# Gate and up by seven Strassen products for each pair of blocks, with half of the conditioning on TensorE, in a two-layer fp32 encoder

## The chip, the cores and the metric

The kernel runs on one core of a Trainium2 chip, once for each launch. The metric is the device time of that launch in microseconds; less is better. Five engines work beside each other, each through its own queue in order: TensorE (PE in the profile; the loads of its stationary operand are PEld), VectorE (DVE), ScalarE (ACT), GpSimd (POOL) and SyncE (SP), which here issues the DMA transfers. They meet only at semaphores.

## The reference, cut to what matters

Two layers over 1024 tokens of width 1024. Each has attention (layer 0, called A, windowed; layer 1, called B, dilated), then a SwiGLU feed-forward part (FFN) with 2816 hidden columns. The conditioning gives each layer six vectors of 1024 numbers (shift, scale and gate for each of the two parts).

```
cond = jax.nn.silu(c)
for i in range(DEPTH):
    mod = (cond @ ada_w[i] + ada_b[i])[:, None, :]
    sh1, sc1, g1, sh2, sc2, g2 = jnp.split(mod, 6, axis=-1)
    h = rmsnorm(x, norm_mix[i]) * (1 + sc1) + sh1
    y = windowed_gqa(...) if i % 2 == 0 else dilated_attention(...)
    x = x + g1 * y
    h = rmsnorm(x, norm_ffn[i]) * (1 + sc2) + sh2
    gate, up = jnp.split(h @ ffn_w_in[i], 2, axis=-1)
    x = x + g2 * ((jax.nn.silu(gate) * up) @ ffn_w_out[i])
return rmsnorm(x, final_norm)
```

## The kernel before

**Numbers.** Every matrix product has fp32 operands, and each is split into two fp32r parts, a high part (a rounding copy) and a low part (what the copy left). A product of a 128x128 block of weights with a 128x512 block of activations is then three matmuls into one PSUM bank (`acc3`, L284 high by high, L285 high by low, L286 low by high). `split_w` splits weights: ACT writes the high half (L180), POOL subtracts it for the low half (L181). Activations are split by ACT and DVE.

**Tiles.** x and h lie transposed, features on partitions, as 8 tiles of 128 features by 512 tokens for each half t of the tokens. The hidden columns are 22 blocks f of 128. For one f and one half, gate and up are 24 matmuls each (`up`, L421). Each f of `down` gives 24 matmuls to each half, in 8 tiles d; blocks of two f (one and three at the ends) share a PSUM bank, and DVE adds the tile to x (`residual`, L354). Down and attention use "d" banks of PSUM, FFN has six of its own beside two.

**Stages.** A start (norm of x, conditioning chunks 0 and 1 of layer 0); a stretch called PRE here (82 to 165 us), in which TensorE makes the last queries, keys and values while DVE forms chunks 2, 3 and 4 (`ada_steps`, L153: one 128x1024 multiply-add for each k; L167 sums over the partitions); attention A (165 to 430), 32 units, each with scores (L490, L491), softmax on DVE and ACT, transposes of the probabilities by TensorE (L532) and the product with the values (L526), into which a hand-written rate (`weave`, `tick`) puts fill work: the queries of half 1, the out-projection, norm and first gate and up of half 0. Then a transition (430 to 625): out-projection of half 1, its norm, gate and up of blocks 1 and 2 for half 0 as cover (`EARLY_A` 3), chunk 5; then FFN A to 1220, in which the 48 accumulations of layer 1's conditioning run on DVE in the background (`step`, one for each tile of gate or up). Attention B, its transition (`EARLY_B` 4) and FFN B repeat this. In `down` of the last block DVE squares the tiles as they come and the next norm starts half by half.

**Norm.** `rms` sums the squares over partitions with four one-column fp32 matmuls (L226), takes a Newton root, and spreads it with four 128-column matmuls (L244). `modulate` then makes each h tile: DVE scales (L256), ACT shifts and rounds (L257), DVE or POOL makes the low part (L262, L260).

**Weights.** `plan` lists the weight tiles in order of use; `weight` fetches ahead as far as there are slots ("w" tiles, two in `main`, a third in FFN). The order on each engine is set when the program is built, by a scheduler that simulates the program and may put instructions of independent pieces in another order than written; pools with few buffers set what can run ahead.

## Time and profile before

| | us |
|---|---|
| median of 3 runs | 2411.71 |
| lowest and highest run | 2411.21, 2413.84 |
| the profiled execution | 2411.33 |
| its span in the trace | 2409.5 |

So 1.8 us of the profiled execution lie outside the span. Below, "busy" is the time in which an engine's datapath worked, "idle before" the gap ahead of an instruction on its engine, and the engine behind an arrow is the one whose semaphore ended that gap. TensorE's matmuls are pipelined, so a matmul's own duration (about 0.39 us for 512 columns) is longer than the distance from one to the next; where matmuls are counted, the distance is what counts. PEclk is the granted clock of TensorE as a share of 2.4 GHz.

### The profile page before, as it was taken

To read this page: it belongs to the slowest core of one execution; us is meant where nothing else is said; L and a number is where in the kernel's file an instruction comes from. 1 tells how busy PE (TensorE), PEld (TensorE's weight loads), DVE (VectorE), ACT (ScalarE), POOL (GpSimd) and SP (SyncE) were. 2 spreads that over 40 slices of the span, in tenths; PEclk is the share of its full clock that TensorE was granted. 3 is DMA by queue.
4 is the path that set the end of the run, shared out by engine and by line. 5 is a ranking of instruction groups with operands and counts; after the bars stand their busy time and mean duration, and the time that the engine had idled before them with its cause. 6 is when DMAs were issued, how large, how long until landed. Compare 5 with 4: busy or idle time off the path is not lost.

```text
span 2409.5 us, 28051 instructions
## 1 busy us (share of the span) xinstructions
PE 2256.8 (94%) x10484; PEld 1863.5 (77%) x10484; DVE 1282.8 (53%) x2265; ACT 881.3 (37%) x1749; POOL 751.4 (31%) x483
## 2 busy tenths in 40 slices
PE   6799898988999999999989999797999999999997
PEld 5687676767788888888879878576788888888886
DVE  8869999578533333333362577786633332222325
ACT  4549887332111111111242788673411111111111
POOL 4525453453122122222233344344431212222210
PEclk9899998999999999999999999898999999999998
DMA  7441123666411111111234765736321111111101
GB/s 281 150 144 36 40 84 132 214 205 219 158 60 39 50 44 53 44 53 44 79 121 155 197 189 179 212 89 202 96 70 53 51 46 53 53 53 44 53 18 70
DMA packets 131224, 248.83 MB, mean 103 GB/s; under 512 B 39312, under 2 KB 66576, under 8 KB 130064
## 3 DMA queue, kind: packets, MB, share of 16 engines
q1 hardware_dynamic: 131088, 247.05, 32.1%
q8 instruction: 82, 1.34, 0.2%
q14 instruction: 54, 0.44, 0.1%
HBM read 214.20 MB, written 30.70 MB: 102 GB/s over the span
## 4 chain that ended last, share of the span: by engine, by line
PE 71%; DVE 16%; DMA 6%; issue 3%; ACT 3%; POOL 1%; SPq 1%; DVEq 0%; ACTq 0%; POOLq 0%
PE ps_d L284 22%; PE ps_d L285 22%; PE ps_d L286 22%; DMA ada_w<-in_ada_w 3%; DVE ada_acc L153 3%; DVE p L493 2%; DVE pp L535 2%; PE ps_o L526 1%; PE ps_t L532 1%; DVE ht L256 1%; DVE p L510 1%; DVE h L262 1%; DMA ml_all<-sd 1%; PE ps_s L491 1%; PE ps_s L490 1%
## 5 line engine op out<-in xcount | busy, mean ns | idle before, releaser
L284 PE MATMUL ps_d<-h,w 128*128 128x512 f32 x1968 | 780.8, 399 | 22.4 <-ACT w L180 11.1
L285 PE MATMUL ps_d<-h,w 128*128 128x512 f32 x1968 | 779.2, 396 | 11.4 <-DVE h L262 9.9
L286 PE MATMUL ps_d<-h,w 128*128 128x512 f32 x1968 | 775.9, 395 | 3.8 <-POOL w L181 3.8
L181 POOL TENSOR_TENSOR w<-raw,w 128x1024 fp32r<-128x1024 f32 (+1 forms) x178 | 431.2, 2424 | 758.7 <-ACT w L180 745.9
L284 PEld LDWEIGHTS ps_d<-h,w 128*128 128x128 f32 x1968 | 374.8, 191 | 96.3 <-ACT w L180 13.7
L285 PEld LDWEIGHTS ps_d<-h,w 128*128 128x128 f32 x1968 | 376.6, 191 | 84.3 <-DVE h L262 12.8
L286 PEld LDWEIGHTS ps_d<-h,w 128*128 128x128 f32 x1968 | 375.3, 191 | 84.7 <-POOL w L181 5.8
L401 DVE TENSOR_TENSOR u<-silu,ps_d 128x512 f32<-128x512 f32 x88 | 60.4, 686 | 607.6 <-PE ps_d L286 591.1
L354 DVE SCALAR_TENSOR_TENSOR x<-ps_d,mod,x 128x512 f32<-128x512 f32 x368 | 270.3, 747 | 149.2 <-PE ps_d L286 149.2
L180 ACT ACTIVATE w<-raw 128x1024 fp32r<-128x1024 f32 (+1 forms) x178 | 185.6, 1046 | 361.2 <-PE ps_d L286 295.3
L284 PE MATMUL ps_d<-act,wo 128*128 128x512 f32 x704 | 275.4, 391 | 8.9 <-DVE x L354 4.8
L286 PE MATMUL ps_d<-act,wo 128*128 128x512 f32 x704 | 274.3, 390 | 0.0
L285 PE MATMUL ps_d<-act,wo 128*128 128x512 f32 x704 | 274.2, 390 | 0.0
L181 POOL TENSOR_TENSOR wo<-raw,wo 128x1024 fp32r<-128x1024 f32 x44 | 105.6, 2399 | 432.7 <-ACT wo L180 425.3
L180 ACT ACTIVATE wo<-raw 128x1024 fp32r<-128x1024 f32 x44 | 46.7, 1060 | 382.8 <-PE ps_d L286 340.2
L284 PEld LDWEIGHTS ps_d<-act,wo 128*128 128x128 f32 x704 | 132.2, 188 | 39.0 <-DVE x L354 6.6
L286 PEld LDWEIGHTS ps_d<-act,wo 128*128 128x128 f32 x704 | 132.2, 188 | 27.5
L285 PEld LDWEIGHTS ps_d<-act,wo 128*128 128x128 f32 x704 | 132.3, 188 | 26.9
L403 DVE TENSOR_TENSOR act<-u,act 128x512 fp32r<-128x512 f32 x88 | 124.8, 1418 | 47.3 <-ACT act L402 47.1
L153 DVE SCALAR_TENSOR_TENSOR ada_acc<-ada_w,cond,ada_acc 128x1024 f32<-128x1024 f32 x70 | 117.2, 1674 | 49.0 <-DMA ada_w<-in_ada_w 48.3
L402 ACT ACTIVATE act<-u 128x512 fp32r<-128x512 f32 x88 | 55.0, 625 | 218.2 <-DVE u L401 218.1
L490 PE MATMUL ps_s<-kh,q 128*128 128x384 f32 (+3 forms) x320 | 104.0, 329 | 21.5 <-DVE stat L493 11.6
(168 smaller groups left out, 2656.3 us busy)
## 6 DMA issues: line engine op xcount, KB each, us to landing
raw<-in_ffn_w_in SPq DMA_DIRECT2D x102, 512.0 KB
ada_w<-in_ada_w SPq DMA_DIRECT2D x80, 512.0 KB
raw<-in_ffn_w_out SPq DMA_DIRECT2D x44, 512.0 KB
raw<-in_b_w_q SPq DMA_DIRECT2D x24, 512.0 KB
qd<-qo SPq DMA_DIRECT2D x48, 256.0 KB
h<-in_ada_w SPq DMA_DIRECT2D x8, 1024.0 KB
raw<-in_a_w_out SPq DMA_DIRECT2D x16, 512.0 KB
q<-qd SPq DMA_DIRECT2D x16, 512.0 KB
```

Source lines behind the costliest of these rows:

```text
L153: nc.vector.scalar_tensor_tensor(acc, w, s, acc, op0=ALU.mult, op1=ALU.add)
L180: self.nc.scalar.activation(w[:, 0], raw, AF.Copy)
L181: self.nc.gpsimd.tensor_tensor(w[:, 1], raw, f32(w[:, 0]), op=ALU.subtract)
L284: mm(ps, lhsT=w[0], rhs=x[0], start=first, stop=False)
L285: mm(ps, lhsT=w[0], rhs=x[1], start=False, stop=False)
L286: mm(ps, lhsT=w[1], rhs=x[0], start=False, stop=last)
L354: self.nc.vector.scalar_tensor_tensor(x, ps, self.mod[:, layer, c * 8 + d:c * 8 + d + 1], x, op0=ALU.mult, op1=ALU.add)
L401: nc.vector.tensor_tensor(u, s, up, op=ALU.mult)
L402: nc.scalar.activation(act[:, 0, halves(t)], u, AF.Copy)
L403: nc.vector.tensor_tensor(act[:, 1, halves(t)], u, f32(act[:, 0, halves(t)]), op=ALU.subtract)
L490: nc.tensor.matmul(ps[:, lo:hi], lhsT=qs[g], rhs=kh, start=True, stop=False)
L493: nc.vector.tensor_tensor_reduce(pt[g][:, lo:hi], ps[:, lo:hi], bias[g][:, lo:hi], -1.0, -NEG if sink is None else sink[1][:, g:g + 1], op ...
```

## The change

**Seven products.** From block 2 on, two blocks f and f+1 are taken together. For gate (and again for up) the result is a 2 by 2 matrix: block f or f+1 by token half 0 or 1; the contraction over 1024 features is cut into two halves of four tiles. That is a 2 by 2 matrix product, which was 8 products of 12 matmuls and becomes 7 (`seven`). The sums of weights that it needs (L502 to L505) are made by DVE in place in the raw tiles before splitting; four split tiles for each seven: w1, w2, w3 of 1024 columns and w4 of 512. The sums of h are made once for each layer in fp32 and split: those of half 0 alone in `sums_first`, the rest with the norm of half 1 (`norm_sums`), 37 DVE instructions in place of 16. The results of the products are added by DVE, partly in place in PSUM (seven additions and one ACT copy for each seven). Five PSUM banks hold products, two hold down tiles, one the accumulator of the background conditioning. The silu-times-up product stays in PSUM, and its low part is taken from there. `down` keeps its matmuls; the weights for it now come as half-width tiles of two blocks (`load_wo`), and there is one such "wo" slot.

**Slots.** In layer A the two "w" slots of `main` are shared with what the plan fetches ahead: the first tile of layer B's key weights is fetched (`w_5377` in the order below) when the last early block has been taken, and is kept to the end of FFN A. The splits w1, w2 and w3 of all sevens of layer A use the other slot. In layer B nothing is left in the plan, and they alternate between two.

**Conditioning.** Chunks 2, 3, 4 and 5 of layer 0 and chunks 1 and 0 of layer 1 are computed by TensorE inside attention A (`ada_blocks`): 24 steps, one for each attention unit, each with 16 fp32 matmuls of 128x128 weights by one column, four weight loads of 256 KB, and one "d" bank. Chunks 2 to 5 of layer 1 stay in the background of FFN A on DVE, as half-width tiles that accumulate in PSUM.

**Cover.** `EARLY` is 2 in both layers (3 and 4 before): in layer A gate and up of block 1, half 0, still stand between the norm's root and its tiles; in layer B they stand before the out-projection, and nothing stands there.

```diff
-EARLY_A = 3
-ORDER_A = "x0 raw act act2 wo aux t2 x1"
+EARLY = 2
+ORDER_A = "x0 raw act wo aux t2 x1 w4 hx"
...
+    def ada_blocks(self, layer, chunks, pool, bufs):
+        nc = self.nc
+        bias = self.vec[:, V_AB + 48 * layer:V_AB + 48 * layer + 48]
+        for j0 in [8 * c + e for c in chunks for e in range(0, 8, 2)]:
+            ps = self.bank()
+            for j in range(2):
+                for k in range(KT):
+                    if k % 4 == 0:
+                        w = pool.tile([P, HT], F, name="ada_w", tag="ada_w", bufs=bufs)
+                        nc.sync.dma_start(w, self.a["ada_blocks"][layer, j0 + j][:, k * P:(k + 4) * P])
+                    nc.tensor.matmul(ps[:, j:j + 1], lhsT=w[:, k % 4 * P:k % 4 * P + P], rhs=self.cond[:, k:k + 1], start=k == 0, stop=k == KT - 1)
...
-        self.banks = deque([(self.psf, "d", 6)])
+        self.banks = deque([(self.psf, "b", 5), (self.psf, "b", 5), (self.psf, "b", 5), (self.psn, "d", 2)])
...
-        self.wslots = deque([(self.main, 2)] * 2 + [(self.paux, 1)])
+        self.wslots = deque([(self.main, 2)] * 2)
...
+    def norm_sums(self, ssq, layer, eng, lows, ups=()):
...
+        rb = self.rms(ssq, eng)
+        for f in ups:
+            self.up(f, 0)
...
+        for k in range(n):
+            x12, x22 = (self.modulate(self.xs[1][i], i, rb, layer, 1, self.pool, h[i], lows[i], keep=True) for i in (k, k + n))
+            b11, b21 = self.b1[k]
+            v(b11, b11, x12, op=ALU.subtract)
+            self.split_h(self.hb[1][k], b11)
+            v(b21, b21, b11, op=ALU.subtract)
+            self.split_h(self.hb[2][k], b21)
+            v(x22, x22, b21, op=ALU.subtract)
+            self.split_h(self.hb[4][k], x22)
+
+    def seven(self, f, gu, use):
...
+        w1 = wt()
+        self.split_w(w1, r[0])
+        w4 = self.pw4.tile([P, 2, HT], R, name="w4", tag="w4", bufs=2)
+        self.split_w(w4, a22)
+        v(a11, a11, a21, op=ALU.subtract)
+        v(a21, a21, a22, op=ALU.add)
+        v(a22, a22, a11, op=ALU.subtract)
+        v(a12, a12, a22, op=ALU.subtract)
+        w2 = wt()
+        self.split_w(w2, r[1])
+        w3 = wt()
+        self.split_w(w3, r[0])
...
+        u = room()
+        nc.scalar.activation(u, product(w1, 0, "12"), AF.Copy)
+        c12 = product(w1, 1, "22")
+        v(c12, c12, u, op=ALU.add)
+        use(0, 1, c12)
+        v(u, product(w2, 1, 2), u, op=ALU.add)
+        p5 = product(w2, 0, 1)
...
-                self.up(f, (1,) if f < early else (0, 1))
-                if i == 0 and prev:
-                    self.down(prev)
...
+        for f in range(early, NF, 2):
+            got = self.gates(f)
+            self.down(f - 2)
+            self.ups(f, got)
+        run(self.bg or ())
...
-            bg = self.ada_steps(0, (2, 3, 4), pre, *PRE_BUFS)
...
+        ada = chain(self.ada_blocks(0, (2, 3, 4), pada, 3), self.ada_blocks(1, (1, 0), pada, 3), self.ada_blocks(0, (5,), pada, 3))
...
+            for _ in range(ADA_A):
+                next(ada, None)
...
-        self.hf[1] = self.norm_half(self.xs[1], ssq, layer, 1, self.pool, nc.vector, LOWS["b_half1"])
-        self.up(3, (0,))
-        return 4
+        self.norm_sums(ssq, layer, nc.vector, LOWS["b_half1"])
+        return EARLY
```

**Attention A on TensorE.** Before, behind the last matmul of a fill tile (`ps_d<-h,w`) stand transposes (L532) and scores (L490):

```order
L284 MATMUL ps_d_1275<-h_670,w_1276 128x512
L285 MATMUL ps_d_1275<-h_670,w_1276 128x512
L286 MATMUL ps_d_1275<-h_670,w_1276 128x512
L532 MATMUL ps_t_1367<-cst_66,p_1297 128x128
L532 MATMUL ps_t_1389<-cst_66,p_1297 128x128
L532 MATMUL ps_t_1367<-cst_66,p_1298 128x128
L532 MATMUL ps_t_1389<-cst_66,p_1298 128x128
```

After, at the same fill product, the first step of the conditioning stands in between (L136; `ps_d_1223` is its bank, `ada_w` its weights, `x4` four matmuls alike):

```order
L292 MATMUL ps_d_1165<-h_670,w_1166 128x512
L136 MATMUL ps_d_1223<-cond_69,ada_w_1224 128x1 x4
L136 MATMUL ps_d_1223<-cond_69,ada_w_1230 128x1 x4
L136 MATMUL ps_d_1223<-cond_69,ada_w_1236 128x1 x4
L675 MATMUL ps_t_1312<-cst_66,p_1190 128x128
L675 MATMUL ps_t_1312<-cst_66,p_1191 128x128
L633 MATMUL ps_s_1327<-kh0_79,q_568 128x384
```

Twelve of the step's 16 one-column matmuls have moved in ahead of the transposes, on the queue that the softmax of the unit waits for; the last four stand behind 15 more rows.

**FFN A on TensorE.** Before, in the steady loop, one tile of gate or up follows the other, and each weight tile (`w_6347`, then `w_6408`) serves both halves; here the seam between the last of half 1 and the first of the next weight:

```order
L284 MATMUL ps_d_6656<-h_4606,w_6347 128x512
L285 MATMUL ps_d_6656<-h_4606,w_6347 128x512
L286 MATMUL ps_d_6656<-h_4606,w_6347 128x512
L284 MATMUL ps_d_6689<-h_4044,w_6408 128x512
L285 MATMUL ps_d_6689<-h_4044,w_6408 128x512
L286 MATMUL ps_d_6689<-h_4044,w_6408 128x512
```

After, at the seam between two sevens (`ps_b` are products, `w_7464` is w3 of one seven, `w_7606` w1 of the next, in the same slot; `ps_d` are down tiles):

```order
L291 MATMUL ps_b_7562<-hx_4823,w_7464 128x512
L292 MATMUL ps_b_7562<-hx_4823,w_7464 128x512
L290 MATMUL ps_d_7748<-act_7559,wo_7745 128x512
L290 MATMUL ps_d_7756<-act_7559,wo_7745 128x512
L290 MATMUL ps_b_7623<-h_5225,w_7606 128x512
L291 MATMUL ps_b_7623<-h_5225,w_7606 128x512
L290 MATMUL ps_b_7640<-h_5227,w_7606 128x512
L291 MATMUL ps_b_7640<-h_5227,w_7606 128x512
L291 MATMUL ps_d_7748<-act_7559,wo_7745 128x512
L292 MATMUL ps_d_7748<-act_7559,wo_7745 128x512
```

The scheduler puts two down matmuls between the last use of `w_7464` and the first use of `w_7606`, and takes the four matmuls with the high part of `w_7606` ahead of those with its low part.

**Layer B, norm of half 1, on TensorE and ACT.** Before, 18 matmuls of a tile of gate and up (`w_13815`, `w_13856`; the first five are shown) stand between the sum over partitions (L226) and the spreading of the root (L244):

```order
L286 MATMUL ps_d_13967<-h_12945,w_13856 128x512
L226 MATMUL ps_d_13896<-ones_68,ssq_13723 128x1 x4
L284 MATMUL ps_d_13966<-h_12945,w_13815 128x512
L285 MATMUL ps_d_13966<-h_12945,w_13815 128x512
L286 MATMUL ps_d_13966<-h_12945,w_13815 128x512
L284 MATMUL ps_d_13967<-h_12945,w_13856 128x512
L285 MATMUL ps_d_13967<-h_12945,w_13856 128x512
```

After, the two stand back to back behind the last matmul of the out-projection, and the first users of the new h follow:

```order
L291 MATMUL ps_d_14651<-h_14298,w_14588 128x512
L292 MATMUL ps_d_14651<-h_14297,w_14588 128x512
L231 MATMUL ps_d_14669<-ones_68,ssq_14501 128x1 x4
L249 MATMUL ps_d_14686<-cst_66,st_14674 128x128 x4
L290 MATMUL ps_d_14781<-h_14691,w_14629 128x512
L290 MATMUL ps_d_14782<-h_14691,w_14771 128x512
```

On ACT before, the weights for the next tiles (L180) are split before the first h tile (L257) of the norm:

```order
L180 ACTIVATE w_13956<-raw_13957 128x1024
L218 ACTIVATE sq_13893<-x1_7_13573 128x512
L230 ACTIVATE st_13901<-ps_d_13896 128x4
L180 ACTIVATE w_13961<-raw_13962 128x1024
L180 ACTIVATE w_14023<-raw_14024 128x1024
L257 ACTIVATE h_13918<-ht_13922,mod_70 128x512
L257 ACTIVATE h_13918<-ht_13926,mod_70 128x512
```

After, the split of a weight that block 1 of half 1 needs (`w_14776`, L184, the former L180) stands behind the last sum of h (`hx`, L440):

```order
L440 ACTIVATE hx_14476<-ht_14738 128x512
L440 ACTIVATE h_13755<-b11_14470 128x512
L440 ACTIVATE hx_14472<-b21_14468 128x512
L440 ACTIVATE hx_14476<-ht_14757 128x512
L184 ACTIVATE w_14776<-raw_14777 128x1024
L408 ACTIVATE silu_14831<-ps_d_14781 128x512
L184 ACTIVATE w_14837<-raw_14838 128x1024
```

The cover has gone from TensorE, and a weight split has moved from ahead of the norm's tiles to behind the last of them on ACT.

## Rows read from the trace of the kernel before

**Rows 1.** The page: busy time by engine, and the chain that ended last.

```profile
PE 2256.8 (94%) x10484; PEld 1863.5 (77%) x10484; DVE 1282.8 (53%) x2265; ACT 881.3 (37%) x1749; POOL 751.4 (31%) x483
...
PE 71%; DVE 16%; DMA 6%; issue 3%; ACT 3%; POOL 1%; SPq 1%; DVEq 0%; ACTq 0%; POOLq 0%
```

**Rows 2.** Windows: stretch, length, busy us by engine, granted clock, DMA.

```profile
82.00:165.00 83.00, 71.91 (x399) 64.47 (x398) 57.78 (x70) 32.85 (x53) 33.92 (x28) 0.87 0.47 157
165.00:430.00 265.00, 241.08 (x1227) 194.84 (x1225) 248.62 (x617) 221.14 (x521) 113.08 (x87) 0.97 0.21 69
430.00:625.00 195.00, 171.15 (x745) 135.27 (x745) 146.41 (x140) 50.22 (x66) 82.78 (x45) 0.97 0.65 218
625.00:1220.00 595.00, 595.00 (x2658) 492.24 (x2657) 209.08 (x256) 108.82 (x147) 129.82 (x56) 1.00 0.18 59
1220.00:1262.00 42.00, 34.99 (x144) 28.60 (x143) 26.10 (x45) 21.48 (x33) 15.59 (x11) 0.88 0.37 122
...
2392.00:2409.50 17.50, 3.94 (x16) 3.56 (x16) 12.89 (x27) 1.00 (x3) 0.00 (x0) 0.57 0.58 218
```

**Rows 3.** Timeline of TensorE in FFN A: start, duration, instruction.

```profile
799.83 0.39 PE L284 MATMUL ps_d<-act,wo 128*128 128x512 f32 x1
...
800.51 0.39 PE L284 MATMUL ps_d<-act,wo 128*128 128x512 f32 x1
```

**Rows 4.** Timeline of TensorE: one-column fp32 products before attention A.

```profile
112.65 3.55 PE L167 MATMUL ps_n<-ones,ada_acc 128*128 128x1 f32 x16 [4.13 <-DVE ht L256]
...
162.90 1.84 PE L167 MATMUL ps_n<-ones,ada_acc 128*128 128x1 f32 x16
164.60 0.37 PE L490 MATMUL ps_s<-kh,q 128*128 128x256 f32 x1
```

**Rows 5.** Lines of TensorE in attention A, 165 to 430: busy, mean ns, idle.

```profile
L526 PE MATMUL ps_o<-pp,vt 128*128 128x512 f32 x176 | 70.1, 436 | 9.4 <-DVE pp L535 8.7 <-ACT pp L534 0.3
L285 PE MATMUL ps_d<-h,w 128*128 128x512 f32 x144 | 58.6, 407 | 1.4 <-DVE h L262 1.4
...
L532 PE MATMUL ps_t<-cst,p 128*128 128x128 f32 x352 | 54.5, 276 | 0.7 <-DVE p L510 0.7
L490 PE MATMUL ps_s<-kh,q 128*128 128x384 f32 (+1 forms) x125 | 46.2, 370 | 9.9 <-DVE ml L493 9.6
```

**Rows 6.** Timeline of TensorE in attention A; windows of attention B, as group 2.

```profile
300.59 0.60 PE L532 MATMUL ps_t<-cst,p 128*128 128x128 f32 x4
300.94 0.47 PE L526 MATMUL ps_o<-pp,vt 128*128 128x512 f32 x1
...
1340.00:1420.00 80.00, 79.79 (x451) 66.50 (x451) 53.45 (x196) 68.09 (x206) 29.57 (x22) 1.00 0.70 193
```

**Rows 7.** The page's groups: residual, and the weight splits (busy, mean, idle).

```profile
L181 POOL TENSOR_TENSOR w<-raw,w 128x1024 fp32r<-128x1024 f32 (+1 forms) x178 | 431.2, 2424 | 758.7 <-ACT w L180 745.9
...
L354 DVE SCALAR_TENSOR_TENSOR x<-ps_d,mod,x 128x512 f32<-128x512 f32 x368 | 270.3, 747 | 149.2 <-PE ps_d L286 149.2
L180 ACT ACTIVATE w<-raw 128x1024 fp32r<-128x1024 f32 (+1 forms) x178 | 185.6, 1046 | 361.2 <-PE ps_d L286 295.3
```

**Rows 8.** Timelines of DVE and POOL in FFN A: two operands in SBUF.

```profile
701.52 0.69 DVE L403 TENSOR_TENSOR act<-u,act 128x512 fp32r<-128x512 f32 x1 [0.70 <-ACT act L402]
...
707.17 2.46 DVE L403 TENSOR_TENSOR act<-u,act 128x512 fp32r<-128x512 f32 x1 [0.97 <-ACT act L402]
...
706.69 2.39 POOL L181 TENSOR_TENSOR w<-raw,w 128x1024 fp32r<-128x1024 f32 x1 [8.49 <-ACT w L180]
```

**Rows 9.** Windows before the out-projection of layer B's second half, as group 2.

```profile
1648.00:1656.00 8.00, 0.00 (x0) 0.00 (x0) 6.98 (x9) 2.15 (x4) 1.64 (x1) 0.64 0.64 166
...
1660.00:1664.00 4.00, 2.90 (x7) 2.35 (x8) 3.97 (x2) 0.72 (x2) 3.83 (x2) 0.50 0.45 124
```

**Rows 10.** Timeline of TensorE in layer B: the norm of the second half.

```profile
1702.67 0.95 PE L226 MATMUL ps_d<-ones,ssq 128*128 128x1 f32 x8
...
1707.70 1.05 PE L244 MATMUL ps_d<-cst,st 128*128 128x128 f32 x8
```

More of the change, by code (lines that the diff above doesn't have):

```diff
@@ L2 @@
 from contextlib import ExitStack
+from itertools import chain
 import concourse.bass as bass
@@ L32 @@
 N_FIRST = 6
[L33 removed]
 BIAS_DVE = 5
[L35 to L38 removed]
+ADA_A = 1
 N_DVE = 5
```

373 lines of the change are left out of this document (202 added, 171 removed).

## The prediction

> **What bounds the kernel now.** I read the shares of the whole span and the chain that ended last, then the stretches, then single instructions. TensorE is busy 94% of the span and is 71% of the chain; no other engine is over 53% [rows 1]. So matmuls that are left out are time, but only where TensorE is what binds. In FFN A it is busy 595.00 of 595 us at clock 1.00, with DVE at 209 and POOL at 130: there nothing else counts, and DVE and POOL have room [rows 2]. In the attention stretch it is busy 241 of 265 while DVE has 249: there DVE binds, and TensorE has a little room [rows 2]. PRE has 72 of 83 at clock 0.87, the transition 171 of 195, the seam between the layers 35 of 42, the tail 4 of 17.5 [rows 2]. The change takes matmuls from the first kind of stretch and puts other ones into the second. Its sum is made against the profiled execution, 2411.33 us, 0.4 under the median.
>
> **The products.** Each pair of blocks has 168 matmuls in place of 192; ten pairs in two layers leave out 480. Three distances between 512-column matmuls are 800.51 - 799.83 = 0.68 us, 0.2267 for one [rows 3]: **-108.8**. This is the largest and the surest term. Down is unchanged in count.
>
> **What keeps TensorE waiting between products.** Layer A has one slot for w1, w2 and w3. At the seam, w1 of the next seven cannot be written before the last matmul on w3 has ended. Then its high half takes 1.05 us on ACT and its low half 2.42 on POOL [rows 7]. TensorE has two down matmuls to put into the first (0.45 us), and four products and four down matmuls in the second (1.81): 0.6 + 0.6 = 1.2 us lost. At the other seam of a pair more down tiles are left to put in, and I get 0.8. Over 20 sevens that is 21 us. Nothing lost is no option with one slot, unless down tiles cover all: 10 at the least. At the most the low half finds POOL at the 1.2 us of w4 or the 2.4 of wo [rows 7]: 60. Between w1 and w2, and w2 and w3, 12 or more matmuls lie in the gap, so these are hidden. Layer B alternates between two slots; I take 5 there (0 to 25), for DVE's additions that free the five product banks: about 30 DVE instructions of 0.7 us in a pair beside 16 residuals of 0.75 [rows 7, 8], 33 us of the pair's 60. Together **+26**. The background sums over partitions become 32 fp32 matmuls, half as many columns each: **+3**.
>
> **A shared port.** A DVE instruction with two operands in SBUF took 0.69 us alone and 2.46 where POOL's 2.39 us subtraction ran beside it (706.69 to 709.08) [rows 8]. The change takes one such instruction from each tile (the low part of the activation now has its operand in PSUM), but adds four weight sums to each seven and makes 28 of the norm's 37 DVE instructions of this kind. By the row a meeting costs up to 1.8 us. I count one or two in each norm, hidden in the estimates below. The Trainium skill, GPSIMD Engine Reference, section Specifications, says that GpSimd shares its SBUF interfaces with VectorE, in contention with VectorE instructions that have two SBUF inputs. By that rule, as a mechanism of this kernel, every one of POOL's subtractions in the two norms holds DVE for its whole length, and it is a rival below.
>
> **Attention A and PRE.** Conditioning goes to TensorE: 24 x 16 = 384 one-column fp32 matmuls. Sixteen records, which are eight such matmuls (two records each), took 164.60 - 162.90 = 1.70 us at full clock, so 0.2125 each, and 3.55 us, 0.44 each, in a stretch at half clock [rows 4]. At full clock that is 81.6 us on TensorE. What does TensorE have now in this stretch? 3 x 144 fill matmuls and 176 of the values [rows 5] at 0.2267 make 137.8; 352 transposes [rows 5] at (300.94 - 300.59)/4 = 0.0875 [rows 6] make 30.8; 251 of the scores [rows 5] at three quarters of 0.2267 make 42.7. Together 211, against 241 busy by durations. With the new ones 293, more than DVE's 249: TensorE becomes the bound here. The stretch cannot be under 293 (+28), and is 347 at most at full clock, if all of it is added (+82). In attention B, where TensorE binds, it is busy 79.79 of 80 us [rows 6], so in the middle of the stretch I expect no idle; of the 24 us of idle now [rows 2] I leave 20, for the first and last units, in which nothing is there to fill. 313, **+48**. The weights are 25 MB more through DMA, 80 GB/s above 69; attention B moves 193 at full clock [rows 2, 6]. SP issues these loads in its one queue with the raw weights; a load that waits for one of three buffers holds the raw tile behind it, and with it a fill tile. In PRE the 24 accumulations on DVE fall away, and with them the column sums. If only idle goes, 83 - 72 = 11 is won; if the clock comes to full too, 72 less 8 of sums, times 0.87, is 56 and 27 is won [rows 2, 4]. I take the middle: **-19**.
>
> **The transitions.** After the root, `norm_sums` has 37 DVE instructions; at 0.69 to 0.75 us each [rows 7, 8] 26 us. Then a weight that is split behind the last copy (1.05) and 48 matmuls (10.9): 38 us from the root to the end of block 1. TensorE has 96 matmuls for that, 21.8. So 16 to 17 us are idle. In layer A the root itself is covered by block 1 of half 0 (10.9 us); with 8 us ahead of and in the out-projection I get 25 of idle where there were 195 - 171 = 24 [rows 2], less the end of chunk 5: **+1** (-8 to +10). In layer B the cover is gone. From the sum over partitions to the spreading it took 1707.70 - 1702.67 = 5.03 us; with the spreading (1.05) [rows 10], the last residual, square and addition ahead, and a scaling and a rounding behind, 9 us. The 18 matmuls that lay beside it were 4.1 us, so 4 were idle. Now 9 + 16 = 25: +21. Longer idle also costs clock: with no matmul in 1648 to 1656, the granted clock was 0.50 still at 1660 to 1664 [rows 9], that is the lower level, 1.2 GHz, after the engine had done nothing. Two gaps with some 4 us each of lost speed behind them, less the one now: +6. **+27** (10 to 38).
>
> **The ends.** The last block of a layer now has two f in place of three as cover for the next norm's first half, 48 matmuls for 72, 5.4 us less. The seam between the layers [rows 2] gets **+5** (0 to 8), the tail, where DVE has 12.9 of 17.5 us [rows 2], **+4** (0 to 7). Three of the new loads stand among those of the start: **+2**.
>
> **Sum.** -109 + 26 + 3 + 48 - 19 + 1 + 27 + 5 + 4 + 2 = -12: **2399 us**. Most of what the products save is given back, in attention A, at the seams and in layer B's transition.
>
> **Rivals.** (1) The work fits better than I count: attention goes to its 293 (20 less), down tiles cover all but 6 us of the seams (20 less), and layer B's idle is half (12 less): 2347. For it: in FFN TensorE had no idle at all [rows 2], and DVE and POOL are half free. Against: one slot in layer A.
> (2) Slower: the seams of layer A. If the low half of w1 waits on POOL for one more subtraction (2.42 us [rows 7]), each of the 20 sevens loses that: +48, 2447. It decides from 1.1 us more at each seam, where 2399 becomes 2421; from 0.6 the gain is gone. For it: a pair has 21.6 us of POOL's subtractions where it had 14.4, and four of them come together.
> (3) Slower: attention A takes all 82: +34, 2433. The conditioning stands in the unit's chain, ahead of its transposes, and DVE, which is full now, waits each time for TensorE; the clock could fall too, and at 0.44 a matmul the price is 170. Against: rows 6, where a full TensorE had clock 1.00.
> (4) The port as the rule of the skill has it: two norms with some 8.7 us of POOL's subtractions each (three of 1.3 and two of 2.4), of which I have 3: +10 to +12, 2410.
> That the change does not leave out the matmuls is excluded: the order has 84 for each seven.
>
> **How the numbers follow.** Forecast 0.36 (its own range 2383 to 2417), rival 1 0.22, rival 2 0.20, rival 3 0.16, rival 4 0.06. Within 0.2% (4.8 us, about what a measurement can tell from no change) means 2407 to 2416.5. Of the forecast's 0.36, 0.24 is faster, 0.09 within, 0.03 slower; rival 1 is all faster; rival 4 is within (0.04) or faster (0.02); rivals 2 and 3 are slower but for 0.01 within. Faster 0.48, same 0.14, slower 0.38. The range from rival 1's near end to rival 2's: 2350 to 2445.
>
> **What would show it.** In the profile after: products' distances of 0.227 and about 480 fewer matmuls in the FFN stretches, 54 us less in each, plus idle of TensorE before the first use of a "w" tile, 1 us each, released by ACT or POOL, in layer A and not in B. Attention A longer by some 48 us with TensorE over 95% busy and DVE under 85%. Layer B with some 25 us of idle after the out-projection, released by DVE, and a clock of 0.50 behind it. PRE some 19 us shorter. Wrong would be: attention A as long as now (then I overrated the fp32 matmuls); idle at the seams in both layers alike (then it is not the slot); idle released by DVE's additions (the product banks).

## The result, and the profile after

The changed kernel takes 2504.59 us in the median of four runs (2503.00 to 2507.26), the kernel before 2412.20 beside it (2411.21 to 2413.84): a ratio of 1.0383, 95% interval 1.0365 to 1.0401. It is 92 us slower, where 12 us faster was forecast, and lies outside the range of 2350 to 2445. The profiled execution took 2503.52, with a span of 2501.7.

First the page of the changed kernel: busy time by engine, and the chain that ended last.

```profile
PE 2295.8 (92%) x10732; PEld 1888.5 (75%) x10732; DVE 1508.5 (60%) x2784; ACT 1000.6 (40%) x1914; POOL 885.3 (35%) x557
...
PE 62%; DVE 12%; issue 9%; POOL 7%; DMA 6%; ACT 3%; SPq 1%; DVEq 0%; POOLq 0%; ACTq 0%
```

Against [rows 1], TensorE is busier in microseconds although 480 long matmuls fewer were issued, and POOL, which was 1% of the chain, is 7%. Now the stretches of the changed kernel that answer to [rows 2]: start and end, length, busy time of PE, PEld, DVE, ACT and POOL, granted clock, DMA share and GB/s. They are attention A with the conditioning in it, the transition of layer A, FFN A, the transition of layer B from ahead of its root, and FFN B.

```profile
170.00:440.00 270.00, 269.28 (x1608) 242.77 (x1608) 190.82 (x474) 160.61 (x377) 83.47 (x57) 0.87 0.39 124
...
581.00:636.00 55.00, 41.72 (x140) 29.51 (x138) 28.75 (x43) 28.48 (x43) 24.90 (x23) 0.75 0.17 54
636.00:1303.00 667.00, 640.16 (x2760) 509.01 (x2760) 378.69 (x543) 162.93 (x217) 219.18 (x101) 0.99 0.23 73
...
1793.00:1851.00 58.00, 32.61 (x114) 23.88 (x115) 33.14 (x58) 25.83 (x40) 17.12 (x8) 0.74 0.11 35
1851.00:2470.00 619.00, 613.39 (x2700) 506.04 (x2698) 336.22 (x480) 159.89 (x210) 221.47 (x100) 1.00 0.16 51
```

Three things stand out. In attention A TensorE is busy 269.28 of 270 us, and yet its clock is 0.87, where it was 0.97 [rows 2]. FFN A has 27 us of idle, where it had none. FFN B is nearly full (613 of 619 us). To place the loss, I cut both traces at events that they share; the 512-column matmuls that each cut has more or fewer are counted at 0.2267 us, and "lost" is the growth beyond that count.

| stretch | before, us | after, us | lost, us | forecast |
|---|---|---|---|---|
| to the first score behind PRE (start and PRE) | 164.6 | 162.6 | -2 | -17 |
| to the norm's sum of half 0 (attention A) | 241.2 | 333.4 | +92 | +48 |
| to the sum of half 1 (out-projection) | 86.1 | 85.1 | 0 | 0 |
| to the next layer's first sum (transition, FFN A) | 714.2 | 722.3 | +58 | +25 |
| seam between the layers and start of B | 105.8 | 114.2 | +12 | +5 |
| attention B | 289.0 | 288.2 | -1 | 0 |
| transition and FFN B | 776.9 | 764.5 | +38 | +32 |
| tail | 31.8 | 31.3 | +4 | +4 |
| 480 matmuls left out | | | -109 | -109 |

The lost column sums to 92 (the parts are rounded). The products saved what was forecast; 201 us were given back, not 97.

**Attention A.** The timeline of TensorE in the changed kernel: start, duration, line, instruction; x8 are eight records, that is four one-column products.

```profile
202.89 1.70 PE L136 MATMUL ps_d<-cond,ada_w 128*128 128x1 f32 x8
204.45 0.77 PE L669 MATMUL ps_o<-pp,vt 128*128 128x512 f32 x1
...
425.01 2.73 PE L136 MATMUL ps_d<-cond,ada_w 128*128 128x1 f32 x24
427.61 0.42 PE L633 MATMUL ps_s<-kh,q 128*128 128x384 f32 x1
```

At 425 us a product costs 2.60/12 = 0.217, as [rows 4] said for the full clock; at 203 us it costs 1.56/4 = 0.39, and the 512-column matmul behind it takes 0.57 to the next. The window of that place shows a granted clock of 0.50, the lower level, 1.2 GHz, in an engine that has waited for nothing; what it did before were products of one column among transposes, scores and values.

```profile
202.89:205.02 2.13, 2.13 (x10) 2.04 (x9) 1.72 (x6) 1.18 (x3) 0.00 (x0) 0.50 0.60 218
```

And the whole stretch from the first score to the norm's sum of half 0, in the kernel before and then in the changed one:

```profile
164.60:405.79 241.19, 221.20 (x1145) 179.37 (x1144) 231.78 (x589) 207.70 (x501) 108.24 (x73) 0.98 0.20 64
```

```profile
162.62:496.04 333.42, 328.23 (x1911) 290.31 (x1910) 249.67 (x619) 213.25 (x502) 108.61 (x73) 0.89 0.38 120
```

TensorE's idle there went from 20.0 us to 5.2. Taken from start to start, less the idle, the records of the products fill 86.3 us, and the other matmuls, as many as before, 241.9 us in place of 221.2: 86.3 + 20.7 - 14.8 = 92.

**The seams of FFN A.** The waits of TensorE from 636 to 1303 us: line, cause, us in all, times, the longest.

```profile
PE ps_b L290 <- ACT w L184: 12.7, 19, 1.2
PE ps_b L292 <- POOL w L185: 7.2, 16, 1.3
PE ps_d L290 <- ACT wo L184: 2.6, 3, 1.2
```

And two of them on the timeline, where they are longest:

```profile
760.97 0.39 PE L292 MATMUL ps_b<-hx,w 128*128 128x512 f32 x1
762.56 0.50 PE L290 MATMUL ps_b<-h,w 128*128 128x512 f32 x1 [1.20 <-ACT w L184]
...
765.01 0.80 PE L292 MATMUL ps_b<-h,w 128*128 128x512 f32 x1 [1.26 <-POOL w L185]
765.60 0.63 PE L290 MATMUL ps_b<-h,w 128*128 128x512 f32 x1
766.03 0.63 PE L291 MATMUL ps_b<-h,w 128*128 128x512 f32 x1
```

The high half of w1 comes 1.20 us late from ACT, the low half 1.26 from POOL, in the way that the prediction described. But most seams are lighter, at 0.3 to 0.6 us for ACT and 0.2 to 0.4 for POOL, like this one:

```profile
1160.86 0.50 PE L290 MATMUL ps_b<-h,w 128*128 128x512 f32 x1 [0.59 <-ACT w L184]
```

Nine waits of 1.2 us between 762 and 858 us make 11 of the 22.5 in the three rows above. Two things more are to be read from the long ones. A wait of 1.20 is 1.59 - 0.227 = 1.36 us between starts, since "idle" begins only when the last matmul's own duration is over. And behind the second wait the distance is 0.43, not 0.227, until 768.16: there the granted clock is 0.50. That is rare, though. The windows of FFN A show the lower level here and once more, at 840 us behind a like pair of waits, and the full clock behind all the other waits, the like pair at 829 and 832 us among them:

```profile
765.00:768.20 3.20, 3.19 (x8) 2.52 (x9) 3.17 (x7) 0.72 (x2) 0.00 (x0) 0.50 0.00 0
768.40:839.90 71.50, 65.84 (x289) 52.88 (x288) 38.11 (x57) 18.26 (x24) 23.83 (x11) 1.00 0.23 74
...
843.50:1303.00 459.50, 443.70 (x1922) 352.10 (x1920) 263.86 (x382) 113.28 (x151) 148.60 (x68) 1.00 0.23 73
```

**Layer B's transition.** The waits of TensorE from 1793 to 1870 us:

```profile
PE ps_d L231 <- DVE ssq L224: 6.9, 1, 6.9
PE ps_d L290 <- ACT h L262: 5.4, 2, 3.8
PE ps_d L291 <- DVE h L265: 4.8, 3, 3.8
PE ps_d L291 <- POOL h L265: 4.6, 1, 4.6
PE ps_d L249 <- DVE st L242: 2.2, 1, 2.2
```

The forecast had 25 us of idle here; these five are 23.9, and the clock from 1793 to 1851 us is 0.74.

### The profile page after: what moved, and what is told of

It reads as the page before. It is cut to its first block, busy times and chain, and to the rows that moved or that the text cites. A ratio compares the mean times of both kernels' runs of the same rounds, so it can differ in the third digit from the quotient of the medians.

```text
span 2501.7 us, 29655 instructions
## 1 busy us (share of the span) xinstructions
PE 2295.8 (92%) x10732; PEld 1888.5 (75%) x10732; DVE 1508.5 (60%) x2784; ACT 1000.6 (40%) x1914; POOL 885.3 (35%) x557
## 3 DMA queue, kind: packets, MB, share of 16 engines
q1 hardware_dynamic: 147376, 243.89, 31.3%
## 4 chain that ended last, share of the span: by engine, by line
PE 62%; DVE 12%; issue 9%; POOL 7%; DMA 6%; ACT 3%; SPq 1%; DVEq 0%; POOLq 0%; ACTq 0%
PE ps_d L290 9%; PE ps_d L292 9%; PE ps_d L291 9%; PE ps_b L292 8%; PE ps_b L290 8%; PE ps_b L291 8%; POOL w L185 5%; PE ps_d L136 3%; PE ps_o L669 2%; PE ps_t L675 2%; DMA ada_w<-in_ada_w 2%; DMA raw<-in_ffn_w_in 2%; DVE ssq L224 1%; PE ps_s L633 1%; PE ps_s L634 1%
## 5 line engine op out<-in xcount | busy, mean ns | idle before, releaser
L185 POOL TENSOR_TENSOR w<-raw,w 128x1024 fp32r<-128x1024 f32 (+1 forms) x254 | 571.7, 2252 | 960.2 <-ACT w L184 935.6
L184 ACT ACTIVATE w<-raw 128x1024 fp32r<-128x1024 f32 (+1 forms) x254 | 249.4, 983 | 534.8 <-PE ps_b L292 237.9
L290 PE MATMUL ps_d<-h,w 128*128 128x512 f32 x688 | 291.5, 431 | 34.6 <-ACT h L262 13.0
L291 PE MATMUL ps_d<-h,w 128*128 128x512 f32 x688 | 289.1, 420 | 24.7 <-DVE h L265 10.9
L292 PE MATMUL ps_d<-h,w 128*128 128x512 f32 x688 | 284.9, 417 | 10.2 <-POOL w L185 10.2
L290 PE MATMUL ps_d<-act,wo 128*128 128x512 f32 x672 | 264.4, 397 | 7.7 <-ACT wo L184 4.2
L291 PE MATMUL ps_d<-act,wo 128*128 128x512 f32 x672 | 262.7, 391 | 0.0
L290 PE MATMUL ps_b<-h,w 128*128 128x512 f32 x640 | 251.9, 394 | 11.5 <-ACT w L184 11.5
L292 PE MATMUL ps_d<-act,wo 128*128 128x512 f32 x672 | 258.3, 391 | 0.0
L292 PE MATMUL ps_b<-h,w 128*128 128x512 f32 x640 | 248.7, 394 | 6.0 <-POOL w L185 6.0
L291 PE MATMUL ps_b<-h,w 128*128 128x512 f32 x640 | 250.0, 391 | 0.0
L290 PE MATMUL ps_b<-hx,w 128*128 128x512 f32 x480 | 188.2, 392 | 2.4 <-ACT w L184 2.4
L292 PE MATMUL ps_b<-hx,w 128*128 128x512 f32 x480 | 187.5, 391 | 1.2 <-POOL w L185 1.2
L290 PEld LDWEIGHTS ps_d<-h,w 128*128 128x128 f32 x688 | 139.0, 204 | 65.7 <-ACT h L262 15.6
L291 PE MATMUL ps_b<-hx,w 128*128 128x512 f32 x480 | 187.3, 390 | 0.0
L291 PEld LDWEIGHTS ps_d<-h,w 128*128 128x128 f32 x688 | 139.7, 203 | 56.1 <-DVE h L265 14.9
L292 PEld LDWEIGHTS ps_d<-h,w 128*128 128x128 f32 x688 | 139.8, 203 | 42.2 <-POOL w L185 13.2
L290 PEld LDWEIGHTS ps_d<-act,wo 128*128 128x128 f32 x672 | 126.0, 188 | 45.7 <-DVE x L360 11.3
L290 PEld LDWEIGHTS ps_b<-h,w 128*128 128x128 f32 x640 | 120.6, 188 | 43.7 <-ACT w L184 19.8
L292 PEld LDWEIGHTS ps_b<-h,w 128*128 128x128 f32 x640 | 120.5, 188 | 37.0 <-POOL w L185 12.5
```

The costliest lines, as they stand in the source:

```text
L184: self.nc.scalar.activation(w[:, 0], raw, AF.Copy)
L185: self.nc.gpsimd.tensor_tensor(w[:, 1], raw, f32(w[:, 0]), op=ALU.subtract)
L290: mm(ps, lhsT=w[0], rhs=x[0], start=first, stop=False)
L291: mm(ps, lhsT=w[0], rhs=x[1], start=False, stop=False)
L292: mm(ps, lhsT=w[1], rhs=x[0], start=False, stop=last)
```

## The experiments

All kernels are edits of the changed one, each run beside the kernel before. The changed kernel is 2504.6 us; differences are from it unless another is named.

| run | us, median | ratio to before, 95% interval |
|---|---|---|
| e1_no_cond | 2404.31 | 0.9962 (0.9948 to 0.9977) |
| e2_quarter | 2445.03 | 1.0131 (1.0110 to 1.0151) |
| e3_wide | 2495.21 | 1.0344 (1.0327 to 1.0362) |
| e4_slot | 2454.33 | 1.0167 (1.0152 to 1.0182) |
| e5_cond_dve | 2434.03 | 1.0094 (1.0076 to 1.0112) |
| e6_order | 2499.92 | 1.0369 (1.0348 to 1.0389) |
| e7_all | 2394.32 | 0.9932 (0.9915 to 0.9948) |
| e8_cols32 | 2487.62 | 1.0316 (1.0298 to 1.0333) |
| e9_cover | 2387.54 | 0.9895 (0.9876 to 0.9914) |
| e10_no_order | 2380.68 | 0.9868 (0.9849 to 0.9888) |
| e11_no_sums | 2356.35 | 0.9770 (0.9753 to 0.9787) |
| e12_no_sums_third | 2348.76 | 0.9746 (0.9723 to 0.9769) |

### Is it the conditioning? (e1_no_cond, e2_quarter)

The theory was that the conditioning on TensorE is the growth of attention A; the rival, that the loads or the order of the queues are. e1 takes the products and the loads out:

```diff
-            ps = self.bank()
-            for j in range(2):
-                for k in range(KT):
...
-            nc.vector.tensor_tensor(self.mod[:, layer, cols], ps[:, 0:2], bias[:, cols], op=ALU.add)
+            nc.vector.tensor_copy(self.mod[:, layer, cols], bias[:, cols])
```

> The changed kernel without the conditioning inside attention A: the 384 one-column products and their 96 loads are left out, and the six chunks of shift, scale and gate are the bias alone. Theory (these products, with the clock that they bring down, are the 90 us by which attention A grew): 2504.6 falls by 85 to 95, to 2410 to 2420, the stretch from 163 us to the norm of half 0 returns from 333 to about 243 us at a clock of 0.97 or more. Rival (the stretch grew through other things of the change, as the order of the queues or the loads of the start): less than 60 us come back, 2445 or more.

e2 keeps every load and one product of four:

```diff
-                    nc.tensor.matmul(ps[:, j:j + 1], lhsT=w[:, k % 4 * P:k % 4 * P + P], rhs=self.cond[:, k:k + 1], start=k == 0, stop=k == KT - 1)
+                    if k % 4 == 0:
+                        nc.tensor.matmul(ps[:, j:j + 1], lhsT=w[:, k % 4 * P:k % 4 * P + P], rhs=self.cond[:, k:k + 1], start=k == 0, stop=k == 4)
```

> The changed kernel with all 96 loads of the conditioning, but one of four one-column products (96 in place of 384; the sums over features are incomplete). Theory products (TensorE's time and clock): three quarters of the way to the run without conditioning, 2430 to 2440. Rival loads (SP's queue, the three buffers, the DMA traffic): within 15 us of the changed kernel, 2490 or more.

Measured: 100 us less without the conditioning (85 to 95 were expected), 60 less with a quarter of its products (65 to 75 were expected). From the first score to the norm of half 0 it is 333.4 us in the changed kernel, 269.2 in e2, 242.1 in e1. The windows from 165 to 390 us of e1 and then of e2:

```profile
165.00:390.00 225.00, 205.74 (x1076) 165.79 (x1073) 218.26 (x543) 194.30 (x464) 103.53 (x68) 1.00 0.20 63
```

```profile
165.00:390.00 225.00, 207.40 (x1145) 175.84 (x1144) 193.51 (x523) 175.33 (x418) 92.69 (x63) 0.96 0.50 157
```

Without the products DVE binds again (218 of 225) at clock 1.00. In e2 neither engine is full, and the clock is already 0.96. So most of the growth is the products, not the loads, and the sum of 92 above leaves nothing for the order of the queues. The loads have a price elsewhere: the first score is at 162.6 us in the changed kernel, 161.6 in e2 with all loads, and 150.9 in e1 with none. Against the 164.6 of before e1 gains 13.7 us, of which 10.2 lie in PRE, counted from the norm's sum at its beginning (86.2 us before, 76.0 in e1). The conditioning's first three loads, which SP issues among those of the start, go with 11 us of loss (e2 against e1), where I had set 2.

### What of it is the clock? (e3_wide, e8_cols32)

e3 turns the product round: the vector is stationary, the weights move.

```diff
-                    nc.tensor.matmul(ps[:, j:j + 1], lhsT=w[:, k % 4 * P:k % 4 * P + P], rhs=self.cond[:, k:k + 1], start=k == 0, stop=k == KT - 1)
+                nc.tensor.matmul(ps[0:1], lhsT=self.cond[:, k:k + 1], rhs=w, start=k == 0, stop=k == KT - 1)
...
+                nc.tensor.matmul(ps[:, j:j + 1], lhsT=row[0:1, j * P:(j + 1) * P], rhs=self.ones[0:1, 0:1], start=True, stop=True)
```

> The changed kernel with the same conditioning on TensorE in another form: the vector is the stationary operand (one column) and the 256 KB of weights move through as 512 columns, 96 fp32 products of 512 columns in place of 384 of one, with 48 small ones behind them; the bytes and the number of loads are the same. By four passes of 0.2133 each that is 96 x 0.85 to 0.91 = 82 to 87 us of TensorE, as much as the 82 of before. Theory clock (one-column products do not hold the clock, 36 of the 90 us): the clock of the stretch rises from 0.86 to 0.97 or more, and the time falls by 25 to 40, to 2465 to 2480. Rival (the clock has another cause, or only TensorE's time counts): within 10 us of 2504.6.

e8 leaves the form and repeats the moving column:

```diff
-                    nc.tensor.matmul(ps[:, j:j + 1], lhsT=w[:, k % 4 * P:k % 4 * P + P], rhs=self.cond[:, k:k + 1], start=k == 0, stop=k == KT - 1)
+                    nc.tensor.matmul(ps[:, 32 * j:32 * j + 32], lhsT=w[:, k % 4 * P:k % 4 * P + P], rhs=self.cond32[:, k], start=k == 0, stop=k == KT - 1)
```

> The changed kernel with 32 equal columns moving in each of the 384 conditioning products in place of one (only the first is read). Theory (one-column products leave the array empty for most of their time, and the clock goes down for it): a product still takes 0.21 us, the clock of 170 to 440 rises from 0.86 to over 0.95 and the time falls by 15 to 25. Rival (the clock falls for another reason): the clock stays at 0.86, and the time stays within 5 us or grows by the longer products.

The window of e3 from 170 to 430 us with one of its product groups, then the window of e8 from 170 to 440 with one of its groups:

```profile
170.00:430.00 260.00, 260.00 (x1113) 148.22 (x1114) 168.97 (x456) 163.91 (x383) 80.25 (x56) 1.00 0.42 127
...
167.25 2.74 PE L133 MATMUL ps_d<-ada_w,cond 128*1 128x512 f32 x6
169.92 0.44 PE L637 MATMUL ps_s<-kh,q 128*128 128x384 f32 x1
```

```profile
170.00:440.00 270.00, 266.60 (x1747) 238.01 (x1746) 211.72 (x534) 181.69 (x428) 95.49 (x64) 1.00 0.43 133
...
302.00 2.76 PE L136 MATMUL ps_d<-cond,ada_w 128*128 128x32 f32 x24
304.60 0.42 PE L633 MATMUL ps_s<-kh,q 128*128 128x384 f32 x1
```

In both the granted clock is 1.00, with TensorE about as full as in the changed kernel at 0.87. In e8 a product costs what it cost (2.60/12 = 0.217 us), and the norm of half 0 is reached at 470.6 in place of 496.0: **25 us of the 92 are the clock**. Of them 4 are the products (82.0 us in all for 86.3); the rest are the other matmuls. Of the whole time 17 us were won, as expected (15 to 25); 7 were lost again in layer B between the norms of its halves (101.1 us for 94.0), where a wait of 10.8 us for a weight's split on ACT stands that the changed kernel does not have. The edit does not touch that place; that the scheduler set its order anew is a guess. e3 fell by 9 only: each wide product took 2.67/3 = 0.89 us as expected, but the 48 small ones behind them took 0.12 for each of their two records, 12 us in all, so that the conditioning became 100 us long where it was 86; the clock paid that back and little more. The forecast of 25 to 40 for e3 left those out.

The Trainium skill, TensorE: Matmul & The Clock Gate, section Part 1, says that the clock's level is set by how busy the engine has been recently. Here the engine is busy 269.28 of 270 us, 260.00 of 260 and 266.60 of 270, and the clock is 0.87, 1.00 and 1.00; the busy time of the profile does not tell the two levels apart.

### The seams (e4_slot)

```diff
-        while len(self.ready) < len(self.wslots) and self.plan:
+        while len(self.ready) < len(self.wslots) and self.plan and not (self.hold and self.plan[0][0][0] == "b"):
```

`hold` is true from the beginning of layer A's FFN to its end, so that nothing of layer B takes the second slot.

> The changed kernel, but no weight of layer B is fetched while FFN A runs, so that the sevens of layer A alternate between two slots as those of layer B do. Theory (the single slot makes the waits at the seams of layer A): the 25 us of waits of TensorE for ACT and POOL between 634 and 1303 us fall under 4, and with the part of each wait that lies inside the last matmul's own duration the time falls by 25 to 34, to 2471 to 2480; up to 5 are lost again where the fetch comes late for layer B. Rival (ACT and POOL are too slow for these splits anyway): under 8 us.

The window of e4's FFN A, and the place that answers to 761 us above:

```profile
634.00:1260.00 626.00, 619.66 (x2756) 511.31 (x2754) 376.24 (x543) 163.79 (x217) 219.25 (x100) 1.00 0.25 78
...
761.85 0.39 PE L293 MATMUL ps_d<-act,wo 128*128 128x512 f32 x1
762.08 0.39 PE L291 MATMUL ps_b<-h,w 128*128 128x512 f32 x1
```

```profile
PE ps_d L291 <- ACT wo L185: 1.6, 1, 1.6
```

50 us less, more than expected. Of the waits for ACT and POOL one of 1.6 us is left, the row above. The stretch from the norm's sum of layer A to the next layer's first sum fell from 722.3 to 680.2 us, that is by 42; another 5 were won between the norms of layer B's halves (89.2 us for 94.0), which the edit does not touch. By the records of the two traces, the 42 are 22 of idle, 7 in the matmuls just ahead of a gap (the part of each wait inside the last matmul's duration), 5 in the first matmuls behind one, 3 at the lower clock, and 5 in the matmuls between. The theory holds; its price was low, since a wait costs about twice the idle that the profile names, and little of that is the clock.

### Conditioning back to DVE (e5_cond_dve)

```diff
-        ada = chain(self.ada_blocks(0, (2, 3, 4), pada, 3), self.ada_blocks(1, (1, 0), pada, 3), self.ada_blocks(0, (5,), pada, 3))
+        ada = self.ada_blocks(0, (5,), pada, 3)
...
+            bg = self.ada_pre((2, 3, 4), pre, 4, 1)
...
-            if b in ("12", "22", 1, 4):
-                self.step()
+            self.step()
...
-            self.bg = None if last else self.ada_steps(self.layers[n + 1], (2, 3, 4, 5), self.paux, ADA_BUFS)
+            self.bg = None if last else self.ada_steps(self.layers[n + 1], (1, 0, 2, 3, 4, 5), self.paux, ADA_BUFS)
```

> The changed kernel with the conditioning taken back from TensorE, but for chunk 5 of layer 0 (64 products in attention A): chunks 2, 3 and 4 of layer 0 are accumulated by DVE in PRE as in the kernel before, and all six chunks of layer 1 in the background of FFN A, one step for each of the seven products. Theory (the move to TensorE cost 100 us and gave nothing in PRE, whose end stood at 163 us in both kernels): attention A returns to 243 to 255 us, PRE still ends at about 163, the background is hidden by the sevens: 2410 to 2425. Rival (DVE has no room for it in PRE or in FFN A with the sevens): 30 us more, 2440 to 2455.

71 us less, and 9 above the expected range. The first score is at 163.6 and the norm of half 0 at 416.7, 253 us of attention A, as expected. PRE, from the norm's sum at its beginning to the first score, in the changed kernel and then in e5:

```profile
83.00:162.60 79.60, 63.06 (x356) 55.86 (x357) 29.04 (x50) 36.73 (x60) 32.06 (x33) 0.87 0.16 49
```

```profile
87.00:163.50 76.50, 69.47 (x404) 61.84 (x404) 56.43 (x70) 33.20 (x55) 34.65 (x31) 0.90 0.48 161
```

DVE is busy twice as long in e5, and PRE is no longer for it. So in this form DVE's accumulations do not pace PRE, and to move them to TensorE won nothing in it. But FFN A with the longer background lost 15 us more than the changed kernel (737.3 for 722.3): the rival had a part. With two slots beside it (e10, below) that part is gone: 682.3, where e4 with the short background has 680.2. So with two slots DVE has the room; the loss came with the single slot.

### The transitions (e6_order, e7_all, e9_cover, e10_no_order)

e6 makes all tiles of h before their sums:

```diff
-        for k in range(n):
-            x12, x22 = (self.modulate(self.xs[1][i], i, rb, layer, 1, self.pool, h[i], lows[i], keep=True) for i in (k, k + n))
...
+        for k in range(n):
+            for i in (k, k + n):
+                self.modulate(self.xs[1][i], i, rb, layer, 1, self.pool, h[i], lows[i])
+        for k in range(n):
+            b11, b21 = self.b1[k]
+            for j in range(2):
+                v(b11, b11, f32(h[k][j]), op=ALU.subtract)
```

> The changed kernel, in which the norm of half 1 first makes all eight tiles of h and only then their sums (45 DVE instructions in place of 37, the first 16 being those of the kernel before). Theory (TensorE waits in both transitions because the h tiles stand among the sums): blocks 0 and 1 of half 1 start as soon as the h tiles are there; the stretch from the root to the first seven falls from 53 us by 12 to 20 in each layer, the idle there from 25 to under 12: 2465 to 2480. Rival (the end of the sums decides, since the sevens need them, or the weights in the two slots do): under 10 us in all.

5 us less, within the noise (the intervals overlap): the theory of e6 fell. The waits of TensorE in its layer B, 1793 to 1850 us:

```profile
PE ps_d L231 <- DVE ssq L224: 8.6, 1, 8.6
PE ps_d L292 <- POOL w L185: 5.8, 1, 5.8
PE ps_d L291 <- DVE h L268: 3.7, 2, 3.0
```

The waits for h are shorter, and a wait for a weight has come in their place: block 1's splits can only start when block 0 leaves the two slots, and then POOL's half of the split runs beside DVE's sums. One such split, and one of the ten DVE instructions of two SBUF operands that were done beside it:

```profile
1823.62 8.43 POOL L185 TENSOR_TENSOR w<-raw,w 128x1024 fp32r<-128x1024 f32 x1 [6.97 <-ACT w L184]
...
1824.35 0.67 DVE L481 TENSOR_TENSOR b<-b,b 128x512 f32<-128x512 f32 x1
```

It took 8.43 us where such a split took 2.42 [rows 7], while the ten took 0.67 each; only the next of them on DVE, at 1830.37 us, took longer, 2.23.

e7 puts the three edits together, e10 leaves the order of the sums as it was, e9 adds to e7 the cover of layer A in layer B:

```diff
-        for f in range(1, EARLY):
-            self.up(f, 0)
         self.ffn_more()
...
-        self.norm_sums(ssq, layer, nc.vector, LOWS["b_half1"])
+        self.norm_sums(ssq, layer, nc.vector, LOWS["b_half1"], range(1, EARLY))
```

> Three edits together: two slots in FFN A, the conditioning back on DVE but for chunk 5, all of h ahead of its sums. If the three causes lie in different stretches, they add: 50 + 85 + 30 less, 2330 to 2350, and so some 3% under the kernel before. If DVE becomes the bound in FFN A (background and sums), or the gains overlap: 2365 or more.

> The three edits together, and in layer B gate and up of block 1, half 0, stand behind the norm's sum in the program, as in layer A, in place of ahead of the out-projection. Theory (the missing cover is half of what layer B's transition lost): 48 matmuls (10.9 us) can lie in the 9 us from the sum to the first h tile, or in the 11 us that TensorE waits for the out-projection's weights; the stretch from the norm of half 0 to the first seven of layer B falls by 5 to 10: 2384 to 2390. Rival (the cover is only moved from one gap to another, since the out-projection waits where it was): within 4 us of the three edits, 2390 to 2398.

> The two larger edits alone: two slots in FFN A, and the conditioning back on DVE but for chunk 5; the sums of h stand among the h tiles as in the changed kernel. If the order of the sums is worth what it was alone (5 us in all), 2396 to 2402. If it was hidden there by the single slot and counts here, 2405 to 2420. The seams and the conditioning alone gave 50 and 70: 2384 if they add without loss.

e10, two slots and the conditioning on DVE, takes 2380.7: 124 less than the changed kernel, where the two edits alone gave 50 and 71. They add, as expected. **It is 1.3% faster than the kernel before** (interval 1.1% to 1.5%), and the best of the complete kernels here. Its attention A and FFN A:

```profile
165.00:417.00 252.00, 236.89 (x1272) 198.19 (x1271) 232.39 (x593) 208.58 (x500) 108.59 (x72) 0.96 0.24 76
...
556.00:1182.00 626.00, 620.75 (x2779) 513.36 (x2777) 393.44 (x577) 165.03 (x220) 218.81 (x100) 1.00 0.29 91
```

With the order of e6 on top (e7, for which 2330 to 2350 were expected) it is 13.6 slower, not faster. The loss lies between the norms of layer B's halves, 101.8 us for the 87.0 of e10. The largest gap there stands in the out-projection:

```profile
1652.21 0.79 PE L323 MATMUL ps_d<-h,w 128*128 128x512 f32 x1 [11.01 <-ACT w L217]
```

In e10 the longest waits there are 3.8 and 3.3 us. All the idle of this part is 32.6 us in e7 and 24.3 in e10, and the clock 0.87 and 0.89; what brought the gap was not tested. e9 is 7 us faster than e7, inside its expected range, but has a wait of 13.8 us in the same place, for tiles of h on ACT in place of a weight. So the run does not settle what the cover is worth. In these three kernels gaps of 4 to 14 us come and go at this place with edits made elsewhere.

### What the sums of h cost (e11_no_sums, e12_no_sums_third)

From e10, the sums are left out of the norm, and then a third weight slot is added in the room that they leave:

```diff
-        for k in range(n):
-            x12, x22 = (self.modulate(self.xs[1][i], i, rb, layer, 1, self.pool, h[i], lows[i], keep=True) for i in (k, k + n))
...
+        self.hb[2], self.hb[4] = h[:n], h[n:]
```

```diff
-        self.wslots = deque([(self.main, 2)] * 2)
+        self.wslots = deque([(self.main, 2)] * 2 + [(self.paux, 1)])
```

> The two edits (slots, conditioning on DVE) with the sums of h left out of the norm of half 1: after the root DVE makes the eight h tiles alone (16 instructions, as in the kernel before), and the products that read the sums read h tiles. Theory (the 37 DVE instructions pace both transitions): from the norm's sum to the end of block 1 of half 1 it was 51 us in layer A and 50 in B for 22 to 33 us of matmuls; without the sums A falls by 10 to 15 and B by 12 to 18, 2348 to 2358 in all. Rival (the weights in two slots, or the root itself, pace them): under 10 us in all, 2371 or more.

> The same without the sums of h in the norm, with a third slot for weights while blocks 0 and 1 of half 1 are made (the room of the sums is free here). If the two slots hold block 1 back by the splits that cannot start before block 0 is done (1.05 on ACT and 2.4 on POOL), 3 to 8 us less than without the third slot, over both layers; if not, within 3.

24 us less, 12.0 in the part of layer A that begins with the norm's sum and 12.7 in that of layer B; and 8 more with the third slot (3.6 and 5.9 in these parts; the intervals of the two runs overlap, so it rests on the parts). The waits of TensorE in layer B, 1670 to 1730 us in e10 and then 1660 to 1720 us in e11:

```profile
PE ps_d L264 <- DVE ssq L257: 8.6, 1, 8.6
...
PE ps_d L324 <- DVE h L298: 4.8, 3, 3.8
PE ps_d L324 <- POOL h L298: 4.6, 1, 4.6
```

```profile
PE ps_d L264 <- DVE ssq L257: 5.8, 1, 5.8
...
PE ps_d L324 <- DVE h L301: 1.4, 2, 0.7
PE ps_d L324 <- POOL h L298: 0.4, 1, 0.4
```

So the sums do pace the transitions, and the two slots seem to hold them behind that; e6, it would follow, gained little because it only put the one in front of the other. A wait for the sum of squares stays, 5.8 us of 8.6.

## Why the prediction was wrong, point by point

- **The products, -109.** Right: 480 matmuls fewer at the same distance.
- **Attention A, +48, measured +92.** This is the step that failed, in two terms of its sum. *The room.* I put TensorE's work of 165 to 430 us at 211, by distances taken from denser places, in place of the 241 that [rows 2] shows busy, and so let 34 of the 82 vanish in its slack. From the first score to the norm of half 0 the 512-column matmuls stood 0.256 us apart, not 0.2267; the slack was the idle alone, 20 us, of which 15 were used. *The clock.* I took the price of a product at the full level, called 347 us the most "at full clock", and kept the half level's 0.44 (0.43 from start to start) out of the range; it cost 25 us (e8), and mostly in the matmuls between: the 512-column ones went from 0.256 to 0.279 us each on average. The products themselves were 86 us against the 82 of the sum. Rival 3 named the place and the clock, but was priced at +34 for the whole and had a chance of 0.16.
- **PRE and start, -17, measured -2.** The reason given for PRE's -19 is not borne out: with DVE's accumulations in it (e5) PRE is 76.5 us, without them 76.0 (e1) and 79.6 (changed kernel), where it was 86.2. What made it shorter in all three was not separated. The conditioning's loads, which came early into the start, cost 11 (e2 against e1), not 2.
- **The seams of layer A, 21, measured 42 (e4).** Mechanism, place and cause right, layer B's seams free of it as the prediction said (0.9 us of waits in 1870 to 2453). The sum of the idle came out right, 22.5 us by the three rows of waits above, but with luck: the usual pair of seams has 0.9 and 0.5 us where 1.2 and 0.8 were forecast, and the cluster of nine long waits, which I did not forecast and no run explains (e4 has none of them), makes up for it. The size failed since a seam also costs what no idle shows, ahead of the gap and behind it.
- **Layer B's transition, +27, measured 38 with FFN B's 5.** Right in kind: the idle was 24 us where 25 were forecast, and the clock 0.74. The sums were 12.7 of it (e11) and the two slots 5.9 (e12, both on top of e10); the rest, root without cover and half clock, was not taken apart.
- **Layer A's transition, +1, and the rest of FFN A.** Of the 58 us lost in layer A after the norm's sum, 42 are the seams; the other 16, against 4 forecast, were not separated but for the sums (12.0 in e11).
- **The seam between the layers, +5, measured 12.** Too low; here too there is a wait of 8.2 us for DVE, and the clock from 1303 to 1358 us is 0.78.
- **The shared port.** Rival 4, in which POOL's subtractions hold DVE through both norms, did not come: in the changed kernel DVE's instructions of two SBUF operands there lost 1.5 us in layer A (1.77 and 1.10 in place of 0.69, at 594 and 596 us) and none in layer B. There it was POOL that ran long: its first low part of an h tile, at 1824.51 us, took 4.49 us, the second 1.27. The Trainium skill, GPSIMD Engine Reference, section Specifications, says that GpSimd's SBUF interfaces are shared with VectorE, in contention when VectorE has two SBUF inputs. The traces agree that the two contend; which of them runs long differs (2.46 for DVE in [rows 8], 8.43 for POOL in e6).

One omission runs through these points: the clock. In the transitions and at the seam between the layers, which got idle, it is 0.74 to 0.78, in attention A, which lost its idle, 0.87; I had charged it once, in layer B's transition.

## What to carry to other kernels

Before work is moved to an engine with slack, take what its queue holds from the distances in that very stretch; distances from a denser one made room here that was not there. Price the clock of the matmuls around the new ones too: products of one column took 21 us that way here, and more columns at the same price gave it back. A reason for a gain wants its own run: PRE was as short with the work in it that had been moved out. And when a new scheme cuts its work into more tiles, look what else sits in the slots it uses: one prefetched tile cost 42 us in its stretch, 50 in all.

## What the hardware showed that was not expected

- With TensorE busy 269.28 us of the 270 from 170 to 440 us the granted clock was 0.87 with one-column fp32 products between the rest; with 32 equal columns in the same products, at the same 0.217 us each, it was 1.00 at 266.60 us busy.
- Two waits of 1.20 and 1.26 us, 2.5 us apart, were followed by some 3 us at a distance of 0.43 us and a granted clock of 0.50; a second such pair was followed by the same, a third one, at 829 and 832 us, by the full clock.
- A weight split on POOL took 8.43 us beside ten DVE instructions of two operands in SBUF, and 2.42 on average in the kernel before; the ten took 0.67 each (e6).
- Turned round, with 512 columns moving, the fp32 product took 0.89 us, and a product with a contraction of one row 0.12 us for each of its two records.
